# Branch B's fillers bound behind their scores, wo's norm from accumulated sums, other PSUM banks for down and wo

## The chip, the core and the metric

The kernel runs on one core of a Trainium2 chip. The metric is the device time of one execution in microseconds (us), lower is better. The kernel before takes 1801.39 us, the median of three runs (1801.26 to 1805.1).

A core has engines that run side by side, each through its own list of instructions in order: TensorE (PE, matmuls and transposes into PSUM banks), VectorE (DVE), ScalarE (ACT), GpSimd (POOL) and SyncE (SP, which issues DMAs). Semaphores make an instruction of one engine wait for one of another.

## What is computed

The reference is a two-layer encoder over 512 tokens of width 1024, all in fp32:

```python
for l in range(DEPTH):                                   # DEPTH = 2
    h = hybrid_mixer(x, ...)                             # branches A, B, C, gates, w_mix_out
    x = layer_norm(ALPHA * x + h, ln1_g[l], ln1_b[l])
    h = memory_cross_attention(x, mem, xwq, xwkv, xwo)   # 4 heads of 128, 256 memory tokens
    x = layer_norm(ALPHA * x + h, ln2_g[l], ln2_b[l])
    h = conv_ffn(x, ...)                                 # up to 2 x 2816, conv of 3, gelu(a) * b, down
    x = layer_norm(ALPHA * x + h, ln3_g[l], ln3_b[l])
```

Inside the mixer, branch B is the dense attention of 8 query heads over 2 key heads, with RMS-normed and rotated q and k:

```python
bq = rope2d(rms_norm(bq)); bk = rope2d(rms_norm(bk))
out_b = softmax(q @ k.T / sqrt(64)) @ v                  # all 512 positions
merged = sum_n (branch_n @ w_branch[n]) * sigmoid(gate_n + b_gate)
```

## The kernel before

**Matmuls.** The precision of fp32 is reached by splitting each operand into a high part (a copy to fp32r, line 133, ACT) and a low part (the rest, line 137, DVE). One product is three matmuls, `mm3` at lines 141 to 144: hi·hi (L142), hi·lo (L143), lo·hi (L144). Weights come in chunks of 128 x 1024 through a ring of raw tiles and five slots of split tiles w; `pump` loads and splits ahead, and a slot comes free when the last step that reads its chunk has run.

**Steps and the scheduler.** `layer` writes a list of steps; each step's `fn` issues its instructions. The scheduler that builds the program may move instructions of different steps past each other (it is run with a model of the engines' times), so the order of a list on PE is not the order of the steps. Two things constrain it: steps marked `urgent` get a higher priority, and an instruction given to `in_order` (`tc.keep_in_program_order`) keeps its place as written. SP's list is written by hand.

**Branch B.** For each of four token tiles t, `q_step` and `kv_step` project q, k and v, `rms` (L535, L536) and the power on POOL (L320) give the norm, L392 and L398 the rotation, L578 and L579 multiply, L133 and L137 split; then `qT_step` (L546) and `kT_step` (L594) transpose with PE, evicted by casts (L551, L595). All keys must be there before the first scores. Then 16 steps u (head u // 2, half of the queries u % 2), each with

- S(u), `bS_step`: for two query tiles q0 and q1 two matmuls into an s bank (two s banks in all), L699; the maximum on DVE (L701); exp on ACT into a ring slot (four slots); a reciprocal; a scaling on POOL
- T(u), `bT_step`: the transposes of the ring slots (L722) into a t bank, split by ACT and DVE into PTb
- PV(u), `bPV_step`: eight matmuls of 256 columns with V (L736); after every second one the pv bank is evicted through o (ACT, L128, then DVE, L666), split into brB.

S(u), T(u) and PV(u) hang on each other through ACT and DVE, so between them stand *fillers*: gate tiles (24 matmuls of 512 columns, acc<-w,xT or acc<-xT,w in the trace, with a Tanh into the ring tile) and branch products (12 matmuls, acc<-brA,w, evicted at L786). `fillers(0, 1)` gives 16 of them for branch A's share, one after each S(u). After the 16 steps come PV(14), T(15) and PV(15), with two gate tiles of branch B's share (`gB[0]`, `gB[1]`) between, then branch B's products (acc<-brB,w).

**wo and the norms.** `wo_step(t)` accumulates the output projection of the cross-attention for one token tile in two halves, each in an acc bank (three acc banks). `residual` (L355) adds it to ALPHA * x and takes bn_stats of the sum (L358); `ln_finish` aggregates (L363), adds the epsilon (L365), takes the power on POOL and applies (x - mean) * g and * rs + b on DVE (L369, L372). Then `xT_step(t)` transposes the tile (L346, two t banks) and splits it for the up projection.

**down and the layer boundary.** The second half of the down projection keeps four token tiles open: tiles 0 and 1 in acc banks, tiles 2 and 3 in the two t banks. The last chunks are done tile by tile (`down_t_step`), then the norm, and `xT_step(0)` and `xT_step(1)` of the next layer, whose transposes need t banks.

Of the kernel before, what the change touches and what calls it, by code (L numbers as in the profile page):

```python
# [10 lines left out]
F32 = mybir.dt.float32  # L11
F32R = mybir.dt.float32r
AF = mybir.ActivationFunctionType
# [3 lines left out]
P = 128  # L17
# [60 lines left out]
def encoder_kernel(ctx: ExitStack, tc: tile.TileContext, x_in, xt_in, mem_in, w_in, pp_in, ln_in, cln_in, ws_in, co_in, out):  # L78
# [27 lines left out]
    def acc_tile(n=512):  # L106
        return ps_acc.tile([P, 512], F32, tag="acc", name="acc")
# [7 lines left out]
    def t_tile(dt=F32):  # L115
        return ps_t.tile([P, 4, P], dt, tag="t", name="t")
# [10 lines left out]
    def act(out, in_, func=AF.Identity, **kw):  # L127
        return nc.scalar.activation(out, in_, func, **kw)  # L128
# [6 lines left out]
    def split_lo(out, in_, hi, scale=None):  # L135
        if scale is None:
            return nc.vector.tensor_tensor(out=out, in0=in_, in1=hi.bitcast(F32), op=ALU.subtract)  # L137
        return nc.vector.scalar_tensor_tensor(out=out, in0=in_, scalar=scale, in1=hi.bitcast(F32),
                                              op0=ALU.mult, op1=ALU.subtract)

    def mm3(ps, lh, ll, rh, rl, first, last):
        nc.tensor.matmul(ps, lhsT=lh, rhs=rh, start=first, stop=False)  # L142
        nc.tensor.matmul(ps, lhsT=lh, rhs=rl, start=False, stop=False)  # L143
        nc.tensor.matmul(ps, lhsT=ll, rhs=rh, start=False, stop=last)  # L144

# [214 lines left out]
    def ln_finish(t, g, b):  # L360
        st = ln_stats.pop(t)
        mv = sm(2, "mv")
        nc.vector.bn_aggr(out=mv, in_=st.rearrange("p a b -> p (a b)"))  # L363
        ve = sm(1, "ve")
        nc.vector.tensor_scalar_add(ve, mv[:, 1:2], LN_EPS)  # L365
        rs = rstd_of(ve, 1, "rs")
        for hf in range(2):
            xt = X[0][:, t, hf * 512:hf * 512 + 512]
            nc.vector.scalar_tensor_tensor(out=xt, in0=xt, scalar=mv[:, 0:1], in1=g[hf], op0=ALU.subtract, op1=ALU.mult)  # L369
        for hf in range(2):  # L370
            xt = X[0][:, t, hf * 512:hf * 512 + 512]
            nc.vector.scalar_tensor_tensor(out=xt, in0=xt, scalar=rs, in1=b[hf], op0=ALU.mult, op1=ALU.add)  # L372
# [33 lines left out]
    def layer(l):  # L406
# [348 lines left out]
        def gate_step(n, m):  # L755
# [8 lines left out]
                R["tg", n, m] = tg  # L764
            return Step(fn, [K("gate", i)])

        def br_step(n, m, stage):
            key = K("br", n * 4 + m // 2)

            def fn():  # L770
                ps = acc_tile()
                w = W.get(key, 2 * 4, P)
                br = R["ABC"[n]]
                for k in range(4):
                    mm3(ps, w[:, 0, (m % 2) * 4 + k, :], w[:, 1, (m % 2) * 4 + k, :],
                        br[:, 0, k, :], br[:, 1, k, :], k == 0, k == 3)
                pump()
                tg = R.pop(("tg", n, m))
                if stage == 0:
                    if m == 0:  # L780
                        R["mg"] = big_tile([P, KD, S], F32, "mg")
                    nc.vector.scalar_tensor_tensor(out=R["mg"][:, m, :], in0=tg, scalar=1.0, in1=ps,
                                                   op0=ALU.add, op1=ALU.mult)
                    return
                mg = R["mg"][:, m, :]
                nc.vector.scalar_tensor_tensor(out=tg, in0=tg, scalar=1.0, in1=ps, op0=ALU.add, op1=ALU.mult)  # L786
                nc.gpsimd.tensor_tensor(out=mg, in0=mg, in1=tg, op=ALU.add)
                if stage == 2:
                    if m == 0:
                        R["mh"] = big_tile([P, KD, S], F32R, "mh")  # L790
                        R["ml"] = big_tile([P, KD, S], F32R, "ml")
                    split_hi(R["mh"][:, m, :], mg, scale=0.5)
                    split_lo(R["ml"][:, m, :], mg, R["mh"][:, m, :], scale=0.5)
            return Step(fn, [key])
# [159 lines left out]
        def wo_step(t):  # L954
            chunks = [K("wo", c) for c in range(4)]

            def fn():
                if t == 0:
                    R["ln"] = load_ln(l, 1)
                ps = [acc_tile(), acc_tile()]  # L960
                sl = slice(t * P, (t + 1) * P)
                oT = R["oT"]
                for half, k in [(0, 0), (0, 1), (0, 2), (1, 0), (1, 1), (1, 2), (0, 3), (1, 3)]:
                    w = W.get(chunks[half * 2 + k // 2], 2, 512)
                    mm3(ps[half], oT[:, 0, k, sl], oT[:, 1, k, sl], w[:, 0, k % 2, :], w[:, 1, k % 2, :],
                        k == 0, k == 3)
                pump()
                for half in range(2):
                    residual(t, half, ps[half])
                ln_finish(t, *R["ln"])  # L970
            return Step(fn, chunks)


# [165 lines left out]
        def down_k_step(half, c):  # L1139
            def fn():  # L1140
                if c == 0:
                    if half == 0:
                        R["dn", 0] = [s_tile(), s_tile(), pv_tile(), acc_tile()]
                        gt = kv_p.tile([P, DM], F32, tag="v", name="ln3g", bufs=2)
                        bt = [p_tile(name="ln3b") for _ in range(2)]
                        R["ln"] = load_ln(l, 2, ([gt[:, :512], gt[:, 512:]], bt))
                    else:
                        R["dn", 1] = [acc_tile() for _ in range(2)] + [
                            t_tile().rearrange("p a b -> p (a b)") for _ in range(2)]
                if half == 0:  # L1150
# [28 lines left out]
        def st(s):  # L1179
            steps.append(s)  # L1180
# [25 lines left out]
                st(tc_step(2 * t - 2))  # L1206
                st(tc_step(2 * t - 1))
        fC, fA, fB = fillers(2, 0), fillers(0, 1), fillers(1, 2)
        for nm, fl in (("a", fC), ("b", fA)):
            if nm == "b":  # L1210
                st(q_step("b", 0))
                st(aT_step(15))
# [16 lines left out]
            for u in range(16):  # L1229
                st(S_(u))  # L1230
                if fl:
                    st(fl.pop(0))
                if nm == "a" and u >= 3 and u % 2 == 1:
                    st(aPV_step((u - 3) // 2))
                if nm == "b" and u >= 2:
                    st(bPV_step(u - 2))
                if u >= 1:
                    st(T_(u - 1))
            for f in fl:
                st(f)  # L1240
        gB = [f for f in fB[0::2]]
        pB = [f for f in fB[1::2]]
        fB = [gB[2]]
        for m in range(8):
            fB.append(pB[m])
            if m + 3 < 8:
                fB.append(gB[m + 3])
        st(gB[0])
        st(bPV_step(14))
        st(bT_step(15))  # L1250
        st(gB[1])
        st(bPV_step(15))
        for f in fB[:6]:
            st(f)
        add(load_x)
# [250 lines left out]
```

## Time and profile before

| | |
|---|---|
| median of three runs | 1801.39 us (1801.26 to 1805.1) |
| the profiled execution | 1802.87 us |
| its span | 1801.1 us |
| mean granted clock of PE | 0.997 |
| PE busy | 1770.0 us, 98% |
| DVE, ACT, POOL busy | 69%, 46%, 14% |

The profile is one execution. Its own time is 1.8 us over its span and 1.5 us over the median. In its rows, out<-in are the names of the tiles that an instruction writes and reads; L numbers are lines of the kernel. A row of the timeline gives start, duration, engine, line, operation, tiles and shapes, and in brackets the idle time of the engine just before with what ended it. A row of the stretches gives the length and then, for PE, PE's weight loads, DVE, ACT and POOL, the busy time and the instructions, then the clock granted to PE, the share of DMA and GB/s.

### The profile page before, as it was taken

The numbers are of one execution on the slowest core, as the hardware profiler recorded it, in microseconds if no ns is written. First come the engines' busy times: TensorE is split into PE (matmuls) and PEld (weight loads), VectorE is DVE, ScalarE is ACT, GpSimd is POOL, SyncE is SP. The second block draws the span as 40 slices with busy tenths as digits, with TensorE's granted clock in tenths as the row PEclk, the third lists the DMA queues.
The fourth block names the chain that finished last, engine by engine and source line by source line (L and its number), as shares of the span: only waits on it lengthen the run. The fifth ranks groups of instructions, "written<-read, shape, count | busy, mean of one in ns | idle before, by whom it ended". The sixth has DMA issues, their size and how long they took to land.

```text
span 1801.1 us, 26334 instructions
## 1 busy us (share of the span) xinstructions
PE 1770.0 (98%) x10081; PEld 1544.4 (86%) x10081; DVE 1247.0 (69%) x2061; ACT 833.6 (46%) x1426; POOL 258.2 (14%) x296
## 2 busy tenths in 40 slices
PE   9999999999999999999999999999999999999998
PEld 7888888878978999988788888888789789998886
DVE  6666856556687898973656668565575878988734
ACT  5355645542444565652223555455424345656520
POOL 2112422121110000000011124321201100000000
PEclk9999999999999999999999999999999999999999
DMA  6222231242423455553412322212333235656421
GB/s 239 94 71 72 70 94 50 68 141 93 154 92 99 128 163 151 163 175 94 151 54 96 92 71 71 82 59 82 118 118 128 82 106 146 164 138 173 133 90 47
DMA packets 63917, 198.79 MB, mean 110 GB/s; under 512 B 7088, under 2 KB 7600, under 8 KB 63536
## 3 DMA queue, kind: packets, MB, share of 16 engines
q1 hardware_dynamic: 53424, 166.20, 28.1%
q0 software_dynamic: 4032, 14.68, 4.8%
q10 hardware_dynamic: 6336, 16.23, 2.7%
q8 instruction: 79, 1.29, 0.3%
q14 instruction: 46, 0.38, 0.1%
HBM read 192.89 MB, written 4.19 MB: 109 GB/s over the span
## 4 chain that ended last, share of the span: by engine, by line
PE 80%; DMA 8%; DVE 7%; issue 3%; ACT 2%; SPq 0%; DVEq 0%; POOLq 0%; ACTq 0%
PE acc L142 19%; PE acc L144 19%; PE acc L143 19%; DMA raw<-in_w_dram 8%; DVE w L137 2%; PE pv L736 2%; PE s L699 2%; PE t L722 1%; DVE cv L1003 1%; PE s L142 1%; PE s L144 1%; PE s L143 1%; DVE cv L1005 1%; PE pv L681 1%; PE s L615 1%
## 5 line engine op out<-in xcount | busy, mean ns | idle before, releaser
L137 DVE TENSOR_TENSOR w<-raw,w 128x1024 fp32r<-128x1024 f32 x308 | 386.2, 1258 | 203.2 <-ACT w L133 198.1
L133 ACT ACTIVATE w<-raw 128x1024 fp32r<-128x1024 f32 x308 | 325.2, 1059 | 387.6 <-PE acc L144 222.0
L144 PE MATMUL acc<-xT,w 128*128 128x512 f32 (+1 forms) x672 | 257.2, 383 | 3.7 <-DVE w L137 3.7
L142 PE MATMUL acc<-xT,w 128*128 128x512 f32 (+1 forms) x672 | 257.1, 384 | 1.1 <-DVE cv L1005 1.1
L143 PE MATMUL acc<-xT,w 128*128 128x512 f32 (+1 forms) x672 | 256.0, 381 | 0.0
L144 PEld LDWEIGHTS acc<-xT,w 128*128 128x128 f32 x672 | 126.4, 188 | 27.5 <-DVE w L137 5.4
L142 PEld LDWEIGHTS acc<-xT,w 128*128 128x128 f32 x672 | 126.2, 188 | 22.1 <-ACT cv L128 1.5
L143 PEld LDWEIGHTS acc<-xT,w 128*128 128x128 f32 x672 | 126.5, 188 | 21.3
L142 PE MATMUL acc<-w,xT 128*128 128x512 f32 (+1 forms) x392 | 139.6, 358 | 1.9 <-ACT w L133 1.5
L144 PE MATMUL acc<-w,xT 128*128 128x512 f32 (+1 forms) x392 | 140.2, 359 | 0.0
L143 PE MATMUL acc<-w,xT 128*128 128x512 f32 (+1 forms) x392 | 139.5, 357 | 0.0
L320 POOL TENSOR_TENSOR rs<-ve,mhalf 128x1 f32<-128x1 f32 x32 | 31.8, 993 | 517.4 <-DVE ve L365 468.0
L1063 PE MATMUL t<-S,w 128*128 128x256 f32 x336 | 95.0, 283 | 0.0
L1064 PE MATMUL t<-S,w 128*128 128x256 f32 x336 | 95.0, 283 | 0.0
L1065 PE MATMUL t<-S,w 128*128 128x256 f32 x336 | 93.7, 283 | 0.0
L701 DVE TENSOR_REDUCE nm<-s 128x1 f32<-128x512 f32 x64 | 44.0, 688 | 64.0 <-PE s L699 63.8
L142 PEld LDWEIGHTS acc<-w,xT 128*128 128x128 f32 x392 | 74.2, 189 | 13.1 <-ACT w L133 2.0
L143 PEld LDWEIGHTS acc<-w,xT 128*128 128x128 f32 x392 | 74.5, 190 | 10.3
L144 PEld LDWEIGHTS acc<-w,xT 128*128 128x128 f32 x392 | 74.3, 190 | 10.1
L203 POOL DMA_DIRECT2D raw<-in_w_dram x28 | 24.7, 882 | 377.9 <-DVE h L1092 115.0
L133 ACT ACTIVATE xT<-t 128x512 fp32r<-128x512 f32 x40 | 22.5, 595 | 109.8 <-PE t L346 109.7
L634 POOL TENSOR_SCALAR ring<-ring,rsm 128x256 f32<-128x256 f32 (+1 forms) x64 | 41.7, 664 | 182.4 <-DVE rsm L632 141.9
(317 smaller groups left out, 4658.7 us busy)
## 6 DMA issues: line engine op xcount, KB each, us to landing
raw<-in_w_dram SPq DMA_DIRECT2D x264, 512.0 KB, 3.6
raw<-in_w_dram SPq DMA_DIRECT2D x56, 256.0 KB, 3.0
raw<-in_w_dram POOLq DMA_DIRECT2D x28, 512.0 KB, 7.2
ub<-in_w_dram SPq DMA_DIRECT2D x28, 256.0 KB, 3.6
lngb<-in_ln_dram ACTq DMA_DIRECT2D x16, 256.0 KB, 4.6
xraw<-in_xt_dram SPq DMA_DIRECT2D x8, 256.0 KB, 6.3
memr<-in_mem_dram ACTq DMA_DIRECT2D x2, 1024.0 KB, 4.8
x<-in_x_dram ACTq DMA_DIRECT2D x4, 512.0 KB, 6.9
```

What stands on the lines that cost most here:

```text
L133: return nc.scalar.activation(out, in_, AF.Copy, scale=scale)
L137: return nc.vector.tensor_tensor(out=out, in0=in_, in1=hi.bitcast(F32), op=ALU.subtract)
L142: nc.tensor.matmul(ps, lhsT=lh, rhs=rh, start=first, stop=False)
L143: nc.tensor.matmul(ps, lhsT=lh, rhs=rl, start=False, stop=False)
L144: nc.tensor.matmul(ps, lhsT=ll, rhs=rh, start=False, stop=last)
L634: nc.gpsimd.tensor_scalar(out=pr_t[qi], in0=pr_t[qi], scalar1=rs[:, qi:qi + 1], scalar2=0.0, op0=ALU.mult, op1=ALU.add)
L699: nc.tensor.matmul(ps, lhsT=R["Q"][:, h, q * P:(q + 1) * P], rhs=R["Kt"][:, kv * 2 + hl, :], start=hl == 0, stop=hl == 1)
L701: nc.vector.tensor_reduce(out=nm[:, qi:qi + 1], in_=ps, axis=AX.X, op=ALU.max, negate=True)
L736: nc.tensor.matmul(ps, lhsT=R["V"][:, kt, h // 4, :], rhs=PT[:, hl, kt, :], start=kt == 0 and hl == 0, stop=kt == NT - 1 and hl == 1, skip ...
L1063: nc.tensor.matmul(o, lhsT=wh, rhs=x(0, k), start=first and k == 0, stop=False, **f)
L1064: nc.tensor.matmul(o, lhsT=wh, rhs=x(1, k), start=False, stop=False, **f)
L1065: nc.tensor.matmul(o, lhsT=wl, rhs=x(0, k), start=False, stop=last and k == 3, **f)
```

## The change

Three edits.

**1. Branch B.** A step wrapped in `behind` sets a flag, and the next first matmul of an `mm3` is given to `in_order`: it keeps its written place behind the scores S(u) that stand ahead of it in the list. In branch B each of the fillers that follows a S(u) is wrapped so. The list of fillers gets one gate tile of branch B's share more (`gB[:1]`), so that each step has one, and at the end `gB[1]` is wrapped too and `gB[2]` is split in two parts of four chunks each (`gate_part`), one ahead of PV(15) and one behind it.

**2. The norm of wo.** The residual's addition gives the sum of its row as a second output (`accum_out`). In place of bn_stats and bn_aggr, ACT squares (x - mean) in two halves with an accumulated sum, and DVE makes the mean and variance from the sums. The two other norms of a layer are as they were.

**3. Banks.** In down's second half tiles 0 and 1 get the t banks, 2 and 3 acc banks. In wo every fourth half (first half of tiles 0 and 2) gets the pv bank in place of an acc bank.

```diff
+    def behind(step):
+        def fn():
+            pinned[0] = True
+            step.fn()
+        return Step(fn, step.chunks)
+
     def mm3(ps, lh, ll, rh, rl, first, last):
-        nc.tensor.matmul(ps, lhsT=lh, rhs=rh, start=first, stop=False)
+        ins = nc.tensor.matmul(ps, lhsT=lh, rhs=rh, start=first, stop=False)
+        if pinned[0]:
+            in_order(ins)
+            pinned[0] = False
...
+    def residual_sum(t, half, ps):
...
+        nc.vector.scalar_tensor_tensor(out=xs, in0=xs, scalar=ALPHA, in1=ps, op0=ALU.mult, op1=ALU.add,
+                                       accum_out=ln_stats[t][:, half:half + 1])
+
+    def ln_finish_sum(t, g, b):
+        st = ln_stats.pop(t)
+        nm, var = st[:, 2:3], st[:, 3:5]
+        nc.vector.tensor_scalar(out=nm, in0=st[:, 0:1], scalar1=st[:, 1:2], scalar2=-1.0 / DM, op0=ALU.add, op1=ALU.mult)
+        for hf in range(2):
+            act(p_tile(name="sq"), X[0][:, t, hf * 512:hf * 512 + 512], AF.Square, bias=nm, accum_out=var[:, hf:hf + 1])
+        ve = sm(1, "ve")
+        nc.vector.tensor_scalar(out=ve, in0=var[:, 0:1], scalar1=var[:, 1:2], scalar2=1.0 / DM, op0=ALU.add, op1=ALU.mult)
+        nc.vector.tensor_scalar_add(ve, ve, LN_EPS)
+        rs = rstd_of(ve, 1, "rs")
...
-                ps = [acc_tile(), acc_tile()]
+                ps = [acc_tile() if (2 * t + i) % 4 else pv_tile() for i in range(2)]
...
-                    residual(t, half, ps[half])
-                ln_finish(t, *R["ln"])
+                    residual_sum(t, half, ps[half])
+                ln_finish_sum(t, *R["ln"])
...
-                        R["dn", 1] = [acc_tile() for _ in range(2)] + [
-                            t_tile().rearrange("p a b -> p (a b)") for _ in range(2)]
+                        R["dn", 1] = [t_tile().rearrange("p a b -> p (a b)") for _ in range(2)] + [
+                            acc_tile() for _ in range(2)]
...
-        for nm, fl in (("a", fC), ("b", fA)):
+        gB, pB = fB[0::2], fB[1::2]
+        for nm, fl in (("a", fC), ("b", fA + gB[:1])):
...
                 if fl:
-                    st(fl.pop(0))
+                    f = fl.pop(0)
+                    st(behind(f) if nm == "b" else f)
...
-        st(gB[0])
+        st(behind(gB[1]))
         st(bPV_step(14))
         st(bT_step(15))
-        st(gB[1])
+        st(behind(gate_part(1, 2, 0)))
         st(bPV_step(15))
+        st(gate_part(1, 2, 1))
```

How this moves PE's instructions, at three places. In the rows, L142, L143 and L144 of the kernel before are L151, L155 and L156 of the changed one; L594 is L630, L699 is L735, L722 is L758, L346 is L358. "x4" is four instructions alike in a row.

At the start of branch B, PE before has this between the transposes of the third and fourth tile of k (ks); brA marks a branch product and acc<-xT,w a gate tile, both fillers:

```order
L594 MATMUL t<-ident_r,ks 128x128 x4
L143 MATMUL acc<-brA,w 128x512
L144 MATMUL acc<-brA,w 128x512
L142 MATMUL acc<-brA,w 128x512
L143 MATMUL acc<-brA,w 128x512
L144 MATMUL acc<-brA,w 128x512
L142 MATMUL acc<-xT,w 128x512
L143 MATMUL acc<-xT,w 128x512
L144 MATMUL acc<-xT,w 128x512
L594 MATMUL t<-ident_r,ks 128x128 x4
```

And the changed kernel has this from the last projection (acc<-xT,w) to the first filler (L582 transposes q):

```order
L156 MATMUL acc<-xT,w 128x512
L582 MATMUL t<-ident_r,qs 128x128 x8
L630 MATMUL t<-ident_r,ks 128x128 x16
L735 MATMUL s<-Kt,Q 128x512 x4
L151 MATMUL acc<-brA,w 128x512
```

All sixteen transposes of k and the first scores now stand in one piece, and every filler that stood among them stands behind.

In a later step of branch B, PE before has this between the transposes of the ring (L722) and the scores of the second query tile (the last row):

```order
L722 MATMUL t<-ident,ring 128x128 x3
L142 MATMUL acc<-brA,w 128x512
L143 MATMUL acc<-brA,w 128x512
L144 MATMUL acc<-brA,w 128x512
L142 MATMUL acc<-brA,w 128x512
L143 MATMUL acc<-brA,w 128x512
L144 MATMUL acc<-brA,w 128x512
L142 MATMUL acc<-xT,w 128x512
L699 MATMUL s<-Kt,Q 128x512 x2
```

And the changed kernel has this at the same kind of place:

```order
L758 MATMUL t<-ident,ring 128x128 x2
L735 MATMUL s<-Kt,Q 128x512 x2
L758 MATMUL t<-ident,ring 128x128 x4
L735 MATMUL s<-Kt,Q 128x512 x2
L151 MATMUL acc<-xT,w 128x512
```

The filler that stood between the two pairs of scores now stands behind both.

At the layer boundary, PE before reaches the first transposes of x within the last matmuls of down's tile 3, which is in a t bank (wa and xT belong to the next layer's first projection):

```order
L143 MATMUL t<-w,gs 128x512
L346 MATMUL t<-ident,x 128x128 x4
L144 MATMUL t<-w,gs 128x512
L142 MATMUL acc<-wa,xT 128x512
L143 MATMUL acc<-wa,xT 128x512
L346 MATMUL t<-ident,x 128x128 x8
```

And the changed kernel has its first transposes of x between down's tiles 2 and 3, both in acc banks now:

```order
L156 MATMUL acc<-w,gs 128x512
L358 MATMUL t<-ident,x 128x128 x8
L151 MATMUL acc<-w,gs 128x512
```

All eight transposes of tile 0 moved ahead of tile 3's 24 matmuls.

More of the change, by code (lines that the diff above doesn't have):

```diff
@@ L139, in split_lo @@
                                               op0=ALU.mult, op1=ALU.subtract)
+    pinned = [False]
+    def behind(step):
[3 more added lines that the diff above has]
+        return Step(fn, step.chunks)
     def mm3(ps, lh, ll, rh, rl, first, last):
-        nc.tensor.matmul(ps, lhsT=lh, rhs=rh, start=first, stop=False)
+        ins = nc.tensor.matmul(ps, lhsT=lh, rhs=rh, start=first, stop=False)
+        if pinned[0]:
+            in_order(ins)
+            pinned[0] = False
         nc.tensor.matmul(ps, lhsT=lh, rhs=rl, start=False, stop=False)
@@ L369, in ln_finish @@
             nc.vector.scalar_tensor_tensor(out=xt, in0=xt, scalar=mv[:, 0:1], in1=g[hf], op0=ALU.subtract, op1=ALU.mult)
+        for hf in range(2):
+            xt = X[0][:, t, hf * 512:hf * 512 + 512]
+            nc.vector.scalar_tensor_tensor(out=xt, in0=xt, scalar=rs, in1=b[hf], op0=ALU.mult, op1=ALU.add)
+    def residual_sum(t, half, ps):
+        xs = X[0][:, t, half * 512:(half + 1) * 512]
+        if half == 0:
+            ln_stats[t] = small.tile([P, 5], F32, tag="lns", name="lns", bufs=4)
+        nc.vector.scalar_tensor_tensor(out=xs, in0=xs, scalar=ALPHA, in1=ps, op0=ALU.mult, op1=ALU.add,
[4 more added lines that the diff above has]
+        nc.vector.tensor_scalar(out=nm, in0=st[:, 0:1], scalar1=st[:, 1:2], scalar2=-1.0 / DM, op0=ALU.add, op1=ALU.mult)
+        for hf in range(2):
+            act(p_tile(name="sq"), X[0][:, t, hf * 512:hf * 512 + 512], AF.Square, bias=nm, accum_out=var[:, hf:hf + 1])
[3 more added lines that the diff above has]
+        rs = rstd_of(ve, 1, "rs")
+        for hf in range(2):
+            xt = X[0][:, t, hf * 512:hf * 512 + 512]
+            nc.vector.scalar_tensor_tensor(out=xt, in0=xt, scalar=nm, in1=g[hf], op0=ALU.add, op1=ALU.mult)
         for hf in range(2):
@@ L765, in gate_step, with gate_part, fn @@
             return Step(fn, [K("gate", i)])
+        def gate_part(n, m, part):
+            i = n * 8 + m
+            def fn():
+                if part == 0:
+                    R["gp"] = acc_tile()
+                ps = R["gp"]
+                w = W.get(K("gate", i), KD, P)
+                for k in range(4 * part, 4 * part + 4):
+                    mm3(ps, w[:, 0, k, :], w[:, 1, k, :], xT[:, :, 0, k, :], xT[:, :, 1, k, :], k == 0, k == KD - 1)
+                pump()
+                if part == 1:
+                    tg = tg_slot(n, m)
+                    act(tg, R.pop("gp"), AF.Tanh, bias=hbias[:, i:i + 1], scale=0.5)
+                    R["tg", n, m] = tg
+            return Step(fn, [K("gate", i)])
         def br_step(n, m, stage):
@@ L1240, in layer @@
                 st(f)
-        gB = [f for f in fB[0::2]]
-        pB = [f for f in fB[1::2]]
-        fB = [gB[2]]
+        fB = []
         for m in range(8):
```

## Prediction

> **What bounds the kernel now.** I began with the page of the profile: busy time of each engine, then the chain that ended last.
>
> ```profile
> span 1801.1 us, 26334 instructions
> PE 1770.0 (98%) x10081; PEld 1544.4 (86%) x10081; DVE 1247.0 (69%) x2061; ACT 833.6 (46%) x1426; POOL 258.2 (14%) x296
> PE 80%; DMA 8%; DVE 7%; issue 3%; ACT 2%; SPq 0%; DVEq 0%; POOLq 0%; ACTq 0%
> ```
>
> TensorE (PE) sets the time: it has 31.1 us without work in 1801.1, and the chain runs through it. The change takes no matmul away and adds none, so it can only close gaps of PE or open new ones. The second view, the waits of PE, says which gaps there are to close:
>
> ```profile
> PE acc L142 <- ACT brB L133: 4.1, 2, 2.1
> PE acc L144 <- DVE w L137: 3.7, 3, 1.7
> PE pv L143 <- DVE xT L137: 2.9, 2, 1.5
> PE t L346 <- DVE x L355: 1.5, 1, 1.5
> PE acc L142 <- DVE x L355: 1.3, 4, 0.3
> PE acc L142 <- DVE ring L786: 0.6, 2, 0.3
> PE pv L736 <- DVE o L666: 0.5, 2, 0.3
> ```
>
> The columns are total us, times and the longest. The brB, ring and o rows are the end of branch B, once in each layer; the x and xT rows are the wo stage and the layer boundary. Everything that the change aims at is in these rows without the w row: 10.9 us in all. A gap that the change opens is weighed against that. The third view is the order in which each engine's instructions stand in the two built programs (shown above); it says where gaps open.
>
> **Start of branch B, in each layer.** Before the first scores S(0), PE must transpose q and k of all four token tiles, and each k passes through VectorE (DVE), ScalarE (ACT) and GpSimd. Before, the scheduler had put fillers (gate and branch A tiles) between these transposes:
>
> ```profile
> 229.29 0.45 PE L546 MATMUL t<-ident_r,qs 128*128 128x128 f32 x4
> 229.58 0.46 PE L142 MATMUL acc<-brA,w 128*128 128x512 f32 x1
> ...
> 237.76 0.46 PE L594 MATMUL t<-ident_r,ks 128*128 128x128 f32 x4
> ...
> 240.66 0.46 PE L594 MATMUL t<-ident_r,ks 128*128 128x128 f32 x4
> 240.96 0.47 PE L143 MATMUL acc<-brA,w 128*128 128x512 f32 x1
> ...
> 248.71 1.07 PE L699 MATMUL s<-Kt,Q 128*128 128x512 f32 x4
> ```
>
> With each filler now bound behind its step's scores, nothing stands between 229.58 and S(0) but 20 transposes in five groups, each 0.3 us (240.66 to 240.96), 1.5 us together. PE works in its written order, so it waits for the chain through the keys. That chain's rows on DVE:
>
> ```profile
> 230.58 1.23 DVE L137 TENSOR_TENSOR w<-raw,w 128x1024 fp32r<-128x1024 f32 x1 [0.22 <-ACT w L133]
> 231.95 0.42 DVE L137 TENSOR_TENSOR ks<-tk,ks 128x256 fp32r<-128x256 f32 x1
> 232.62 0.69 DVE L786 SCALAR_TENSOR_TENSOR ring<-ring,acc 128x512 f32<-128x512 f32 x1 [0.24 <-PE acc L144]
> 235.58 0.29 DVE L579 TENSOR_TENSOR tk<-tk,rs 128x128 f32<-128x128 f32 x1 [0.69 <-POOL rs L320]
> 236.65 0.41 DVE L137 TENSOR_TENSOR ks<-tk,ks 128x256 fp32r<-128x256 f32 x1
> 238.26 0.69 DVE L595 CAST Kt<-t 128x512 fp32r<-128x512 f32 x1 [1.20 <-PE t L594]
> ```
>
> The last key is ready at 237.06 (236.65 + 0.41). It waited for no filler's matmuls except through L786, which now comes later; in its place two casts of Kt (0.69 each) stand in DVE's row, so I take 237.1 to 237.3. Then a group of transposes and the handover (0.5 us, as from the group at 237.76 to its cast at 238.26), the cast 0.69 and a handover of 0.1 to 0.2: S(0) at about 238.6. PE then idles 238.6 - 229.58 - 1.5 = 7.5 us in each layer: **+15.0**. The fillers that stood there are not saved; they run later. Bounds: without the w row (1.23), the L786 row and the longer waits around them S(0) could come near 235.7 (4.6 us idle); with one more piece of 0.8 us in the chain, 8.3 us.
>
> **The clock after such a gap.** How PE's clock answers to idleness shows once in this trace, at the start (stretches: PE busy, then other engines, PEclk ahead of the last two columns; then rows of PE):
>
> ```profile
> 7.00:8.00 1.00, 0.61 (x2) 0.30 (x2) 1.00 (x2) 0.63 (x1) 0.00 (x0) 0.91 0.94 344
> 8.00:9.00 1.00, 1.00 (x3) 0.81 (x4) 0.88 (x2) 0.57 (x1) 0.00 (x0) 0.50 1.08 367
> 11.00:12.00 1.00, 1.00 (x5) 0.84 (x4) 0.95 (x2) 0.61 (x1) 0.00 (x0) 0.88 1.07 432
> ...
> 6.47 1.01 PE L142 MATMUL acc<-w,xT 128*128 128x512 f32 x2 [1.47 <-ACT w L133]
> 9.33 0.63 PE L142 MATMUL acc<-w,xT 128*128 128x512 f32 x1
> 9.75 0.63 PE L143 MATMUL acc<-w,xT 128*128 128x512 f32 x1
> 12.50 0.39 PE L142 MATMUL acc<-w,xT 128*128 128x512 f32 x1
> 12.73 0.39 PE L143 MATMUL acc<-w,xT 128*128 128x512 f32 x1
> ```
>
> After a stretch with an idle 1.47 us in it the granted clock was 0.50 from about 7.8 to 11.2 (0.91 and 0.88 in the mixed microseconds), 3.4 us, and matmuls of 512 columns followed each other by 0.42 us (9.33, 9.75) where 0.23 (12.50, 12.73) is usual. If a gap of 7.5 us does the same, eight matmuls at 0.42 lose 8 x 0.19 = 1.6 us in each layer: **+3.2**. Bounds: nothing, and two such stretches, +6.4.
>
> [...]
>
> **Steady state of branch B.** The order now sets T (second half of the step before), scores of the first half, T, scores of the second half, with no filler between; before, three to seven and more matmuls of fillers stood ahead of the second scores. There are two score banks; the second scores need the exp of the step before on that bank, and this exp needs its ring slot, which that T has just read:
>
> ```profile
> 306.75 0.49 PE L722 MATMUL t<-ident,ring 128*128 128x128 f32 x3
> 307.00 0.48 PE L699 MATMUL s<-Kt,Q 128*128 128x512 f32 x1
> ...
> 307.01 0.59 ACT L128 ACTIVATE o<-pv 64x512 f32<-64x512 f32 x1 [5.15 <-PE pv L736]
> 307.63 0.69 ACT L128 ACTIVATE ring<-s,nm 128x512 f32<-128x512 f32 x1
> 308.22 0.19 ACT L128 ACTIVATION_READ_ACCUMULATOR ring<-s,nm 128x1 f32 x1
> ```
>
> The last of the three T starts at about 306.86; the exp ends at 308.32 (307.63 + 0.69), 1.5 us later, with the eviction o (0.59) ahead of it on ACT, and about 1.1 without. PE gets there in 0.9: two score matmuls (2 x 0.23) and four transposes (0.45). So it waits 0.57 in the six steps that have o and some 0.16 in two others: 3.7 us in a layer. Besides, in the new ACT order a weight split waits, in one or two steps, for a slot that PE frees at a filler's end, with an exp queued behind it on ACT and the scores behind that; between 0 and 3 us, of which I take 0.7, since each such split is only about 1 us long. 4.4 in each layer: **+8.8**; bounds 2 and 8 in each. Before, PE's waits list nothing of this kind, so there is nothing to win there.
>
> **End of branch B.** The stretch from the last scores to the first tiles of branch B, in layer 0 (PE busy is the first number behind the length):
>
> ```profile
> 358.65:376.22 17.57, 14.73 (x83) 11.53 (x82) 10.57 (x15) 8.72 (x14) 4.12 (x4) 1.00 0.28 97
> ```
>
> PE lacks work for 2.84 us here, most of it the brB row's 2.06 (4.1 over two). Two gate tiles (48 matmuls) and part of a third now stand ahead of PV(15) and behind it, 5.4 us each, longer than the chain they cover. The transposes of the last step still wait for exp and ring; I leave 0.6. Gain 2.2 in each layer: **-4.4** (bounds -2 and -6.4).
>
> **Layer boundary, once.** The first xT step needs two t banks, and before, down's tile 3 held one:
>
> ```profile
> 897.96 0.50 PE L142 MATMUL acc<-wa,xT 128*128 128x512 f32 x1 [0.45 <-ACT xT L133]
> 900.21 1.32 PE L346 MATMUL t<-ident,x 128*128 128x128 f32 x8 [1.52 <-DVE x L355]
> ```
>
> Now tiles 0 and 1 hold them, whose residuals are done by then, and a whole down tile (24 matmuls) covers the split. Both waits go: **-2.0** (0 to -3.2).
>
> **Norm of the wo stage.** Per tile two bn_stats and an aggregate leave DVE, two Square passes with a sum go to ACT, and two small scalar steps come in:
>
> ```profile
> 892.37 0.69 DVE L358 BATCH_NORM_STATS2 bn<-x 128x6 f32<-128x512 f32 x1
> ```
>
> DVE is rid of about 2 x 0.69 a tile; a Square of that width, not in the trace, I estimate by the exp row with its read, 0.69 + 0.19, two a tile on an ACT that is 46% busy. But the Squares wait for the residual's sum and the scaling on DVE waits for the Squares, so the chain of one tile is no shorter. The bank swap takes the 0.3 us wait of wo (x row, four times) down a little, while xT(0) now stands behind all of wo's matmuls. I take -0.5 in each layer: **-1.0**, bounds -5 (all xT and x rows) and +4.
>
> **Sum.** 15.0 + 3.2 + 8.8 - 4.4 - 2.0 - 1.0 = +19.6. The profiled execution took 1802.87 us, 1.5 over the median of the three runs (1801.39); so 1822.5 by the profiled run, and **1821.0** against the median.
>
> **Rivals.** (1) Only the gaps at the start count: no slower clock, no waits in the steady state, all gains in full: 15.0 - 4.4 - 2.0 - 1.0 = +7.6, 1809. For it: waits on ACT as short as 0.6 may fall together with others. Against it: the order leaves no cover.
> (2) Faster: the chain through the keys is short as soon as DVE and ACT are rid of the fillers' evictions and splits. S(0) then comes at 235.7 in both layers, with 4.6 us idle, and the same relief takes o and the splits out of the exps' way: 9.2 with no steady waits, against gains at their ends (6.4 + 3.2 + 5.0 = 14.6): -5.4, 1796. It decides once start and steady state together cost less than the gains. Against it: POOL's 0.69 and the DVE rows of one token tile after another are the chain itself, and w's split is still in DVE's order ahead of ks.
> (3) No change: costs at their low ends (9.2 at the start, 4 in the steady state, no slow clock) meet gains near their high ends (11 to 14.6): 1799 to 1804.
> (4) The splits on ACT hold up the scores in every second step: 8 in each layer for 4.4, and the norm stage loses its 4: 19.6 + 7.2 + 5.0 = about +32, 1833 to 1834.
> (5) The slow clock lasts twice as long, about 6.8 us behind each gap, as PE resumes in the middle of a stretch that was already idle: sixteen matmuls at 0.42, 3.2 in each layer, so +22.8 in all, 1824. For it: at the start the clock fell at 7.8, after work had resumed at 6.47, so it follows its own stretches. Against it: there, one stretch was enough. [...]
>
> **Numbers.** Forecast (1811 to 1832) 0.51, the first rival 0.13, the fourth 0.06, the fifth 0.13: slower 0.83. The second, 0.10, is faster. The third, 0.07, lies within 0.2%, 3.6 us, which is about what a measurement of this kernel can tell from none. The range, 1803 to 1834, leaves out the faster case and the far ends.
>
> **What would show it.** Right: PE idle 7 to 8 us ahead of the first score matmuls of branch B, once in each layer, a granted clock of 0.50 behind each, waits of s on ACT's exp in later steps, and rows of brB and of t on x gone. The forecast is wrong if that first gap is under 4.6 us, or if the span grows elsewhere than between the first k transposes and the last exp of branch B.

## The result, and the profile after

The changed kernel takes 1816.87 us (median of four runs, 1814.23 to 1820.74) against 1801.46 us before: ratio 1.0087, 95% interval [1.0071, 1.0103], so 12.8 to 18.6 us slower. The forecast was 1821.0 with a range of 1803 to 1834. The profiled execution took 1814.23 us, its span 1812.5.

The page of the changed kernel, busy times and the chain that ended last:

```profile
span 1812.5 us, 26335 instructions
PE 1775.4 (98%) x10081; PEld 1547.4 (85%) x10081; DVE 1233.1 (68%) x2069; ACT 842.9 (47%) x1458; POOL 253.4 (14%) x296
PE 83%; DVE 7%; DMA 5%; issue 3%; ACT 2%; SPq 0%; POOL 0%; DVEq 0%; POOLq 0%; ACTq 0%
```

The matmuls are the same 10081; PE is without work for 37.1 us instead of 31.1, and its busy time grew by 5.4 us with no more work in it, at a mean granted clock of 0.993 instead of 0.997. The waits of PE in the changed kernel (us in total, times, longest):

```profile
PE t L630 <- ACT ks L133: 6.1, 2, 3.2
PE s L735 <- ACT ring L128: 5.6, 16, 0.4
PE t L358 <- DVE xT L137: 2.6, 2, 1.3
PE pv L772 <- ACT PTb L133: 2.4, 2, 1.2
PE t L630 <- DVE Q L587: 1.6, 2, 0.8
PE s L735 <- DVE Kt L631: 1.6, 2, 0.8
PE t L630 <- DVE Kt L631: 1.4, 2, 0.7
```

The old rows of brB, ring L786, o and x are gone. In their place stand two new families: transposes of k that wait for the chain through the keys (ks, Q, Kt), and 16 waits of scores on the exp into the ring. New are also the waits of PV on PTb at the end of branch B and of the transposes of x on the split xT in wo. The timeline of PE at the start of branch B in layer 0:

```profile
227.61 0.80 PE L582 MATMUL t<-ident_r,qs 128*128 128x128 f32 x8
229.20 0.54 PE L630 MATMUL t<-ident_r,ks 128*128 128x128 f32 x4 [0.79 <-DVE Q L587]
229.99 0.54 PE L630 MATMUL t<-ident_r,ks 128*128 128x128 f32 x4 [0.25 <-ACT Q L133]
231.22 0.86 PE L630 MATMUL t<-ident_r,ks 128*128 128x128 f32 x4 [0.70 <-DVE Kt L631]
235.06 1.08 PE L630 MATMUL t<-ident_r,ks 128*128 128x128 f32 x4 [2.98 <-ACT ks L133]
236.93 2.08 PE L735 MATMUL s<-Kt,Q 128*128 128x512 f32 x4 [0.78 <-DVE Kt L631]
238.80 0.63 PE L151 MATMUL acc<-brA,w 128*128 128x512 f32 x1
239.23 0.63 PE L155 MATMUL acc<-brA,w 128*128 128x512 f32 x1
...
241.81 0.39 PE L156 MATMUL acc<-brA,w 128*128 128x512 f32 x1
242.04 0.39 PE L151 MATMUL acc<-brA,w 128*128 128x512 f32 x1
```

From the transposes of q to S(0) pass 236.93 - 227.61 = 9.32 us, 5.5 of them shown as idle, the rest transposes that grew longer towards the end (1.08 us for four, 0.45 before). The rows behind S(0) show the clock: 0.43 us from matmul to matmul at 238.80, 0.23 at 241.81. The stretches around it in layer 0, then in layer 1 (the granted clock is the number ahead of the last two):

```profile
228.00:231.00 3.00, 1.49 (x13) 1.06 (x12) 2.55 (x5) 2.41 (x5) 0.35 (x1) 1.00 0.01 3
231.00:234.00 3.00, 0.86 (x4) 0.61 (x4) 2.53 (x10) 0.00 (x0) 0.52 (x1) 0.51 0.48 180
...
237.00:240.00 3.00, 3.00 (x7) 2.44 (x8) 1.38 (x2) 1.01 (x3) 0.00 (x0) 0.50 0.00 0
240.00:243.00 3.00, 3.00 (x12) 2.38 (x11) 0.25 (x2) 0.55 (x2) 1.36 (x2) 0.79 0.00 0
...
1132.00:1135.00 3.00, 0.41 (x2) 0.23 (x2) 1.68 (x6) 0.42 (x1) 0.69 (x1) 0.53 0.21 83
...
1138.00:1141.00 3.00, 3.00 (x9) 2.35 (x8) 1.17 (x3) 1.56 (x4) 0.65 (x1) 0.50 0.00 0
1141.00:1144.00 3.00, 3.00 (x11) 2.41 (x11) 0.87 (x2) 0.00 (x0) 0.81 (x3) 0.77 0.00 0
```

Worked out from the mixed stretches (0.51, 0.79; 0.53, 0.77), the clock is halved from 231.1 to 241.3 and from 1132.2 to 1142.4: 10.2 us both times, three times the 3.4 us seen at the kernel's start before.

Where the time went, as lengths of stretches between the starts of the same matmuls in both profiles (us):

| stretch of PE | before | changed | growth |
|---|---|---|---|
| layer 0, transposes of the last q to the first mix matmul (229.29 to 406.14, 227.61 to 415.92) | 176.85 | 188.31 | +11.5 |
| layer 1, the same | 176.84 | 189.02 | +12.2 |
| layer 0, first wo matmul to the last of the first up tiles | 54.39 | 54.13 | -0.3 |
| layer 1, the same | 55.61 | 54.12 | -1.5 |
| layer boundary, 200 matmuls from the 5001st on | 44.53 | 41.83 | -2.7 |
| all others: kernel's start, up and down stages | | | -7.8 |

Between the ends of each stretch of branch B PE has the same 896 matmuls in both kernels. The first five add up to +19.2. The others, in which instructions stand in the order of before, are taken up below.

### The profile page after: what moved, and what is told of

Read it like the earlier page. It is cut to its first block, busy times and chain, and to the rows that moved or that the text cites. A ratio compares the mean times of both kernels' runs of the same rounds, so it can differ in the third digit from the quotient of the medians.

```text
span 1812.5 us, 26335 instructions
## 1 busy us (share of the span) xinstructions
PE 1775.4 (98%) x10081; PEld 1547.4 (85%) x10081; DVE 1233.1 (68%) x2069; ACT 842.9 (47%) x1458; POOL 253.4 (14%) x296
## 4 chain that ended last, share of the span: by engine, by line
PE 83%; DVE 7%; DMA 5%; issue 3%; ACT 2%; SPq 0%; POOL 0%; DVEq 0%; POOLq 0%; ACTq 0%
PE acc L151 19%; PE acc L155 18%; PE acc L156 18%; DMA raw<-in_w_dram 5%; PE s L735 2%; PE pv L772 2%; DVE w L137 2%; PE t L1117 1%; PE t L1116 1%; PE t L1118 1%; PE s L155 1%; PE s L156 1%; PE s L151 1%; PE t L155 1%; PE t L151 1%
## 5 line engine op out<-in xcount | busy, mean ns | idle before, releaser
L151 PE MATMUL acc<-xT,w 128*128 128x512 f32 (+1 forms) x672 | 256.2, 382 | 0.7 <-DVE cv L1058 0.7
L156 PE MATMUL acc<-xT,w 128*128 128x512 f32 (+1 forms) x672 | 255.7, 381 | 0.6 <-DVE w L137 0.6
L155 PE MATMUL acc<-xT,w 128*128 128x512 f32 (+1 forms) x672 | 256.2, 382 | 0.0
L156 PEld LDWEIGHTS acc<-xT,w 128*128 128x128 f32 x672 | 126.4, 188 | 23.5 <-DVE w L137 1.1
L151 PEld LDWEIGHTS acc<-xT,w 128*128 128x128 f32 x672 | 126.2, 188 | 22.5 <-ACT cv L128 1.0
L155 PEld LDWEIGHTS acc<-xT,w 128*128 128x128 f32 x672 | 126.5, 188 | 21.7
L151 PE MATMUL acc<-w,xT 128*128 128x512 f32 (+1 forms) x392 | 139.1, 356 | 1.3 <-ACT w L133 0.9
L156 PE MATMUL acc<-w,xT 128*128 128x512 f32 (+1 forms) x392 | 139.7, 358 | 0.0
L155 PE MATMUL acc<-w,xT 128*128 128x512 f32 (+1 forms) x392 | 138.7, 355 | 0.0
L151 PEld LDWEIGHTS acc<-w,xT 128*128 128x128 f32 x392 | 74.0, 189 | 12.9 <-ACT w L133 1.9
L155 PEld LDWEIGHTS acc<-w,xT 128*128 128x128 f32 x392 | 74.0, 189 | 10.1
L156 PEld LDWEIGHTS acc<-w,xT 128*128 128x128 f32 x392 | 73.9, 189 | 10.0
L128 ACT ACTIVATE ring<-s,nm 128x512 f32<-128x512 f32 x64 | 44.3, 692 | 64.9 <-PE t L758 44.3
L1116 PEld LDWEIGHTS t<-S,w 128*128 128x128 f32 x336 | 64.5, 192 | 0.5
```

The source lines that it names most:

```text
L151: ins = nc.tensor.matmul(ps, lhsT=lh, rhs=rh, start=first, stop=False)
L1116: nc.tensor.matmul(o, lhsT=wh, rhs=x(0, k), start=first and k == 0, stop=False, **f)
```

## Experiments

Two theories were to be told apart. **A**, the forecast's: the loss is made in branch B by the pins, in three parts: the gap ahead of S(0), the slow clock behind it, and scores that wait on an exp with nothing in between; the other edits gain. **Rivals**: the other edits lose too, the rearranged list and not the pin is to blame, or the slowness has another cause. Times are medians; a ratio is to the runs of before on the same chip.

**Branch B's edit alone.** Norm and banks as before:

```diff
-                ps = [acc_tile() if (2 * t + i) % 4 else pv_tile() for i in range(2)]
+                ps = [acc_tile(), acc_tile()]
...
-                    residual_sum(t, half, ps[half])
-                ln_finish_sum(t, *R["ln"])
+                    residual(t, half, ps[half])
+                ln_finish(t, *R["ln"])
...
-                        R["dn", 1] = [t_tile().rearrange("p a b -> p (a b)") for _ in range(2)] + [
-                            acc_tile() for _ in range(2)]
+                        R["dn", 1] = [acc_tile() for _ in range(2)] + [
+                            t_tile().rearrange("p a b -> p (a b)") for _ in range(2)]
```

> Only edit 1, branch B's list and pins; norm and banks as before. Theory A (the loss lies in branch B: gap at its start, slow clock behind it, waits on exp): both branch B stages lose 11 to 13 us each as in the changed kernel, and the -2 to -4 of the other edits is missing, so 1817 to 1824, +18 to +22. Rival R (part of the loss comes from the Square passes of the norm on ScalarE or from the other banks): the time falls below 1813.

Measured: 1826.72 us, ratio 1.0134 [1.0114, 1.0154], 24.6 us above the 1802.12 of before there. This is 2.7 over theory A's upper end and far from the rival: the other edits don't lose. Its two stretches of branch B take 188.3 and 188.8 us, as in the changed kernel.

**The other two edits alone.** Branch B's list as before:

> Edits 2 and 3 alone, branch B as before. Theory A: the 2.0 us of idle time at the layer boundary go and wo gains 0 to 1 in each layer: -2 to -4, 1797.5 to 1799.5, and no gap at the start of branch B. Rival R: no faster than before, 1801 or more, since two Square passes per tile delay wo's norm.

Measured: 1797.12 us, ratio 0.9970 [0.9956, 0.9984]: 5.0 us faster, 1 more than expected at the upper end, with the interval reaching from 2.9 to 7.9. The layer boundary is 2.70 us shorter, as in the changed kernel.

**The changed list without pins.**

```diff
-                    st(behind(f) if nm == "b" else f)
+                    st(behind(f) if nm == "b" and False else f)
...
-        st(behind(gB[1]))
+        st(gB[1])
...
-        st(behind(gate_part(1, 2, 0)))
+        st(gate_part(1, 2, 0))
```

> The changed kernel without any pin: the list with one gate tile more and the split gate tile stay, but no filler is bound. Theory A (the pins make the loss, since the fillers that covered the key chain can no longer move ahead): no gap over 1 us at the start of branch B, the idle time at branch B's end back at 2 to 3 us in each layer, and 1797 to 1801. Rival L (the rearranged list, not the pin, moves the fillers): the gap at the start stays and the time is over 1808.

Measured: 1800.11 us, ratio 0.9993 [0.9982, 1.0004]. PE again has fillers between the transposes, and S(0) to S(1) is 6.35 us, as before at a granted clock of 1.00, so the pin is the cause and not the list. But from the last scores to the first mix matmul it takes 50.1 us in each layer where the kernel before takes 47.3. As many gate matmuls stand behind the last scores as before (76); what differs is the order of T and PV among them. PE waits 4.4 us there in layer 0 (358 to 377 us), not the 2 to 3 expected, where before has 2.7, and the granted clock is 0.72 from 372 to 378 us, which is 3.4 us at half, where before has 1.00. So the list alone makes branch B's end 2.9 us worse. With that the -5 of the other edits is nearly used up.

**The clock by itself.** Between the transposes of k stand short matmuls of a constant, whose results are overwritten:

```diff
+        def warm(n):
+            def fn():
+                ps, z = s_tile(), ident.bitcast(mybir.dt.bfloat16)
+                for _ in range(n):
+                    in_order(nc.tensor.matmul(ps[:, 0:256], lhsT=z[:, 0:P], rhs=z[:, 0:256], start=True, stop=True))
+            return Step(fn)
...
                     st(kT_step(t - 1))
+                    if nm == "b" and t > 1:
+                        st(warm(6 if t == 2 else 22))
             st(fl.pop(0))
             st(kT_step(3))
+            if nm == "b":
+                st(warm(5))
```

> The changed kernel with 33 short matmuls of constants (256 columns) placed among the key transposes, so that TensorE is not idle in the gap; their results are overwritten, nothing else is moved. It measures the clock's share alone. Theory A: the first scores start at the same time (within 0.6 us), the granted clock stays at 1.00 there, the 12 + 4 matmuls behind the gap take 3.7 us instead of 5.8, and the time falls by 2 to 3 us in each layer against the changed kernel: 1811 to 1813, with less spread from run to run. Rival W (the slowness behind the gap is not the clock's, or the clock falls all the same): 1815 or more.

The stretch with the gap and PE from S(0) on in layer 0, then two stretches of layer 1, in this run:

```profile
235.00:238.00 3.00, 2.33 (x22) 1.84 (x19) 1.81 (x9) 0.41 (x1) 0.69 (x1) 1.00 0.42 157
...
239.75 1.19 PE L735 MATMUL s<-Kt,Q 128*128 128x512 f32 x4 [0.22 <-DVE Kt L631]
240.78 0.39 PE L151 MATMUL acc<-brA,w 128*128 128x512 f32 x1
...
243.52 1.07 PE L735 MATMUL s<-Kt,Q 128*128 128x512 f32 x4
...
1135.00:1138.00 3.00, 2.97 (x19) 1.99 (x17) 2.81 (x10) 0.00 (x0) 0.24 (x1) 0.68 0.53 175
1138.00:1141.00 3.00, 3.00 (x23) 2.29 (x21) 1.11 (x3) 0.42 (x1) 0.46 (x1) 0.76 0.00 0
```

In layer 0 the clock stays at 1.00. In layer 1 it is halved once, worked out from the two mixed stretches from 1136.1 to 1139.4, among the short matmuls, and full again ahead of S(0) at 1141.35. With a full clock behind the gap S(0) to S(1) takes 243.52 - 239.75 = 3.77 us, in layer 1 3.76, where the changed kernel has 5.79 and 6.57; everything from S(1) to the last scores is the same to 0.05 us. So the halved clock costs 2.0 us in one layer and 2.8 in the other. S(0) comes 9.14 us after the transposes of q instead of 9.32 (layer 1: 9.46 instead of 9.31): the gap itself has almost nothing to do with the clock.

The whole time did not show the gain: 1816.52, ratio 1.0075 [1.0055, 1.0096], not told apart from 1.0087 and 3.5 us over theory A's upper end. By its number rival W would hold, and its second half did happen once, in layer 1; but wherever the clock was full the slowness behind the gap was gone. The profiled execution, the slowest of the four, shows where the gain went. Against the changed kernel's profile branch B takes 2.2 us less in layer 0 and only 1.0 less in layer 1, where its end holds another 3.4 us of half clock (1255.5 to 1258.9); the kernel's start and the wo, up and down stages, where nothing differs, take 8.7 us more. In layer 0's up and down stage PE waits 4.1 us (2.4 of them on one split of w), in the changed kernel's 0.5.

**Pinned behind the first scores only.** Each step's scores are two steps now, and the filler is bound between them:

```diff
-                st(S_(u))
-                if fl:
-                    f = fl.pop(0)
-                    st(behind(f) if nm == "b" else f)
+                if nm == "b":
+                    st(bS_half(u, 0))
+                    st(behind(fl.pop(0)))
+                    st(bS_half(u, 1))
...
```

> The changed kernel with each step's filler bound behind the first query tile's scores instead of both, so that filler work can lie between the two. It tests the cost in the steady state. Theory A (the second scores wait on the exp that the transposes before them release, with nothing in between): the 16 waits of 0.37 us of scores on ScalarE's exp go, first scores of step 1 to last scores of step 15 falls from 99.5 us to 96.5 to 97 in each layer, the gap and the slow clock at the start stay (S(0) to S(1) again 5.5 to 6.6 us): 1810 to 1813. Rival B (the scores wait for their PSUM bank and not for what stands between): the waits stay, 1815 or more.

Measured: 1805.55 us, ratio 1.0016 [1.0006, 1.0027], 11 us faster than the changed kernel and about twice the gain that theory A had said. The waits of PE in this kernel from S(0) of layer 0 to its mix stage:

```profile
PE s L735 <- DVE Kt L631: 0.8, 1, 0.8
PE pv L775 <- DVE PTb L137: 0.4, 1, 0.4
PE pv L775 <- ACT PTb L133: 0.3, 1, 0.3
PE t L761 <- DVE PTb L137: 0.2, 1, 0.2
```

And the same stretch of the changed kernel:

```profile
PE s L735 <- ACT ring L128: 2.8, 8, 0.4
PE pv L772 <- ACT PTb L133: 1.2, 1, 1.2
PE s L735 <- DVE Kt L631: 0.8, 1, 0.8
PE pv L772 <- DVE PTb L137: 0.3, 1, 0.3
```

The eight waits on exp are gone. From S(1) to the first mix matmul this kernel takes 167.83 us, the changed one 173.20: 5.4 less in each layer. What the eight waits cost can be read from the starts of matmuls in the changed kernel:

```profile
267.89 0.60 PE L758 MATMUL t<-ident,ring 128*128 128x128 f32 x4
268.86 0.72 PE L735 MATMUL s<-Kt,Q 128*128 128x512 f32 x2 [0.37 <-ACT ring L128]
```

From the start of the four transposes to the start of the scores pass 0.97 us; at 254.11, where the scores do not wait, 0.35. So this wait costs 0.62 us, not 0.37. A single transpose has a row of 0.27 us, but a score that does not wait starts 0.03 us after the start of the transpose ahead of it (249.41 and 249.44); the idle time in brackets counts only from the end of the transposes' row (267.89 + 0.60 = 268.49, and 0.37 to 268.86). All eight cost 4.75 us in a layer, where the view shows 2.8. The waits at the end of branch B, read in the same way, cost 2.04 us in the changed kernel and 1.55 here, which makes 5.2 of the 5.4. My mistake was in the expectation, which took the shown waits for the whole cost. That the time from S(1) to the last scores did not get shorter (100.2 against 99.5) is no contradiction, since more filler lies ahead of the last scores now. In layer 1 the slow clock lasted only 6.8 us here (1129.5 to 1136.4), which is part of the gain in time.

**Two fillers left free at the start.** On top of that, 36 matmuls may move ahead of the last key, and one more gate tile is taken into the list:

```diff
-        for nm, fl in (("a", fC), ("b", fA + gB[:1])):
+        for nm, fl in (("a", fC), ("b", fA + gB[:2])):
...
-            st(fl.pop(0))
+            for _ in range(3 if nm == "b" else 1):
+                st(fl.pop(0))
             st(kT_step(3))
...
-        st(behind(gB[1]))
+        st(behind(gB[2]))
-        st(behind(gate_part(1, 2, 0)))
+        st(behind(gate_part(1, 3, 0)))
```

> As the run before, with two fillers (36 matmuls, 8.2 us) left unbound ahead of the last key transposes, and one gate tile of branch B's share more in the list, so that 15 steps still have a filler and two gate tiles are kept for the end. Theory A (what the start needs is cover for 7.5 us, the rest of the fillers is free to be bound): under 1 us idle at the start, clock 1.00, no waits on exp but in the last, unfilled step (1 us), end of branch B as in the changed kernel, so against before 2.7 us at the boundary, some 0.7 in wo and 1 to 2.5 in branch B: 1794 to 1797.5. Rival C (the fillers that stood at the start were all needed there): 1800 or more.

> As the run before with three fillers (48 matmuls, 11 us) left unbound at the start and two steps near the end without one. Theory A: no gap at the start, 2 to 3 us of waits in the two unfilled steps in each layer: 1796 to 1800, 1 to 4 slower than the run before. Rival C: faster than the run before by 2 or more.

> The version with two unbound fillers at the start once more, on the chip of the two others: 1794 to 1797. Theory A: 1 to 1.5 us slower than the same with acc banks in wo; rival E: 1 us or more faster than that.

Measured: 1795.24 us with two free fillers, ratio 0.9955 [0.9943, 0.9968], and on another chip 1793.89, 0.9952 [0.9934, 0.9969]; with three 1795.31, 0.9953 [0.9938, 0.9968]. Both beat the kernel before and the changed one; between two and three there is no difference, against the expectation of 1 to 4 us. PE's waits in branch B with two free fillers (225 to 425 us):

```profile
PE s L735 <- DVE Kt L631: 1.0, 1, 1.0
PE pv L775 <- DVE PTb L137: 0.9, 1, 0.9
PE t L761 <- POOL ring L747: 0.6, 1, 0.6
PE pv L775 <- ACT PTb L133: 0.4, 1, 0.4
```

The gap of 7.5 us is 1.0, the mean granted clock 0.998 where the changed kernel has 0.993, and 36 matmuls of cover are enough, not the 75 of before. Yet from the last transpose of q to mix branch B takes 173.4 us (405.90 - 232.47), before 173.5 (406.14 - 232.63): its 2.9 us of waits stand where before had 2.7. By these two profiles branch B gains nothing by pins, even good ones; what this version has over the kernel before comes from the other two edits. One small thing may speak for the pins: in three of the ten stretches of branch B in kernels with the old list and no pins, a 3.4-us piece of half clock at the end made it 1.1 to 1.4 us longer, in none of the eight with free fillers and pins. Such small numbers do not show it.

**The norm alone, and wo's banks.**

> Only the norm of wo from accumulated sums, all banks and branch B as before; one look, read from the trace from wo's first matmul to the up projection. Theory A (the Square passes have room on ScalarE, and the chain of a tile is no shorter): that stretch within 0.7 us of before, each Square 0.6 to 0.7 us and an accumulator read of 0.2. Rival D (the norm alone brings wo's gain): 1 us or more shorter in each layer.

The waits of PE in wo and xT, with the norm alone (505 to 560 us):

```profile
PE acc L151 <- DVE x L390: 0.9, 2, 0.6
PE pv L151 <- ACT xT L133: 0.5, 2, 0.3
PE pv L155 <- DVE xT L137: 0.2, 1, 0.2
```

And in the changed kernel with the pv bank (515 to 567 us):

```profile
PE t L358 <- DVE xT L137: 1.3, 1, 1.3
PE pv L155 <- DVE xT L137: 0.6, 1, 0.6
PE pv L151 <- ACT xT L133: 0.2, 1, 0.2
```

The Square passes take 0.716 us each with a read of 0.188. From wo's first matmul to the last of the first up tiles it takes 53.37 and 53.42 us, before 54.39 and 55.61, and with branch B's edit alone 55.89 and 54.43. In the kernel before, layer 1's stretch holds a piece of half clock:

```profile
1433.00:1436.00 3.00, 1.22 (x5) 1.02 (x6) 3.00 (x6) 0.00 (x0) 0.00 (x0) 0.77 0.00 0
1436.00:1439.00 3.00, 3.00 (x19) 3.00 (x19) 2.93 (x7) 0.00 (x0) 0.92 (x1) 0.67 0.00 0
```

That is 3.4 us at half, from 1434.6 to 1438.0, and the 55.89 has such a piece too (553.2 to 556.6). So the norm brings 1.0 by the waits, which is rival D, and the one run took 1797.02 us. Another 1.2 to 1.5 us come where it spares the slow clock: of the six stretches with the old norm (three kernels) four hold such a piece, of the 22 with the norm from sums (eleven kernels) none. With the pv bank the stretch is 54.13: the bank swap moves the transposes of x behind all of wo, where they wait for a t bank (1.3 us, the first of the rows above for the changed kernel), and gives 0.7 us back in each layer.

> The version with two unbound fillers at the start and the pins behind the first scores, but wo's halves in acc banks as before; norm from sums and down's banks as changed. Theory A (in wo the sums gain and the pv bank gives it back: the look at the norm alone had TensorE waiting 1.6 us in wo and xT where the changed kernel has 2.1 and before had 2.7): wo's first matmul to the first up tiles 0.5 to 0.8 us shorter in each layer than with the pv bank, so 1 to 1.5 us faster than that version, 1793 to 1795. Rival E (the pv bank is what brings wo's gain): 1 us or more slower than that version.

> The norm from sums and down's banks alone, wo in acc banks, branch B as before. Theory A: against before -2.7 at the boundary and -1.0 in wo in each layer: 1796 to 1798.5. Rival E: 1799 or more.

Measured: 1792.10 us, ratio 0.9954 [0.9937, 0.9970], for the version with two free fillers and acc banks in wo, and 1795.31, 0.9961 [0.9945, 0.9976], for norm and down's banks alone. The stretch is 53.36 and 53.42 us with acc banks, 54.11 and 54.15 with the pv bank, as theory A has it; the 1.5 us in all do not stand out of the intervals of the whole time (0.9954 against 0.9952).

**down's banks alone, and the waits of the up stage.**

> Only down's banks as changed; norm, wo and branch B as before. It tells whether the shorter waits of the up projection, in profiles of kernels with the norm from sums 1.6 to 6.3 us of TensorE waits in both layers against 7.2 and 7.4 in two without it, come from the norm or from chance. Both theories: 2.7 us less at the layer boundary. Theory N (the norm's relief of VectorE reaches the weight splits of the up projection): waits of the up and down stretches (560 to 885 and 1455 to 1800 us) at 6 us or more, time 1799 to 1801. Rival Z (chance between runs): waits 2 to 5 us as in the others, 1796 to 1799.

Measured: 1799.80 us, ratio 0.9990 [0.9977, 1.0003], and 2.72 us less at the boundary. The waits in the two up and down stretches are 3.1 us, not 6 or more. That is rival Z's number while the time is theory N's. Of the 7.4 of branch B's edit alone, 2.6 were waits of its wo stage, which lies later there and reached into the window; and the run with short matmuls, which has the new norm, had 6.3. So these waits vary by chance, and the norm as their cause is not shown. What the old norm does cost here is in the wo stage: 55.91 and 55.90 us, both layers with a piece of half clock.

## Why the prediction was right

**The gap at the start**, +15.0: S(0) was put 9.31 us behind the transposes of q (238.6 - 229.29); it came 9.32 behind them, in layer 1 9.31. The chain held: in the changed kernel's DVE list casts of Kt took the place of the L786 row and of a cast of Q, and the w split stayed.

```profile
229.26 1.22 DVE L137 TENSOR_TENSOR w<-raw,w 128x1024 fp32r<-128x1024 f32 x1
230.39 0.68 DVE L631 CAST Kt<-t 128x512 fp32r<-128x512 f32 x1
230.99 0.41 DVE L137 TENSOR_TENSOR ks<-tk,ks 128x256 fp32r<-128x256 f32 x1
...
235.04 0.42 DVE L137 TENSOR_TENSOR ks<-tk,ks 128x256 fp32r<-128x256 f32 x1 [0.54 <-ACT ks L133]
236.18 0.69 DVE L631 CAST Kt<-t 128x512 fp32r<-128x512 f32 x1 [0.72 <-PE t L630]
```

Rival (2), a chain that shrinks once the fillers' work is out of the way, fell with this: S(0) would have come 6.4 us after the transposes.

**The clock**, +3.2: direction right, size too small. The granted clock was 0.50 behind each gap as forecast, but for longer than the 3.4 us that it took over from the kernel's start: S(0) at 236.93 still had 4.4 us of slow clock ahead, S(0) at 1136.36 6.0 us, since they came at different points of two stretches of the same length. The two layers pay 2.0 and 2.8, together 4.8. Rival (5) had 6.8 us of slow clock behind each gap, and half of the 3.2 us that it adds came. The prediction said that the clock's answer shows once in the profile before; it shows a second time, in wo (1434.6 to 1438.0, the rows above). There it fell within an idle 1.47 us, and the work that resumed at 1435.16 had 2.8 us of slow clock left, not 3.4: in these cases the cost went with the point at which the work resumed.

**The steady state**, +8.8: eight waits in each layer were forecast, six longer and two shorter, and so they came; by the starts they cost 4.75 in each layer, 9.5. Six have the eviction o ahead of the exp on ACT, as forecast, and cost 0.61 to 0.68 each, not 0.57. In the two others a weight split that had waited 3.8 us for PE and a Tanh stand ahead of the exp without a gap (in layer 0 at 289.62, 290.59 and 291.16): that is the head-of-line wait of the forecast, and they cost 0.47 each, where it had 0.16 each and 0.7 besides. So the mechanism was right, the six 0.4 too small in a layer and the rest 0.1 too large.

**The end of branch B**, -4.4: by the starts of matmuls, as for the eight waits (what a step from start to start takes beyond the usual one between two such matmuls), PE loses 4.05 us behind the last scores in the kernel before and 2.04 in the changed one, in each layer, so -4.0. In the view 1.5 us of waits are left in layer 0 (the two rows of PV on PTb), not the 0.6 that the prediction left. By subtraction, 11.5 - 7.5 - 2.0 - 4.75 + 2.0 = -0.75 in layer 0 and 12.2 - 7.5 - 2.8 - 4.75 + 2.0 = -0.85 in layer 1 remain: 1.6 us that branch B gains somewhere else, and where is not shown.

**The boundary**, -2.0: -2.7, the same in every kernel with down's banks changed; a wait of 0.45 and one of 1.52 cost more than they show, as above. **wo**, -1.0: -0.3 and -1.5, of which 1.2 is the piece of half clock that only the kernel before has; the step was right that the Squares and the scaling wait for one another, but wrong that the bank swap helps, and it left out the clock.

**The sum.** 15.0 + 4.8 + 9.5 - 4.0 - 1.6 - 2.7 - 1.8 = +19.2 by stages, +19.6 in the forecast. Single terms were off by up to 1.6 us, in both directions; that their sum comes within 0.4 is luck in part. The time grew by 15.4, interval 12.8 to 18.6. The other stretches of the profiled execution add -7.8 to its growth, which makes it 11.4: the kernel's start 1.7, the rest in the up and down stages. In the fourteen profiles of this document's kernels the start (to the transposes of the last q) takes 227.6 to 230.6 us with the same matmuls, the up and down stage 321.1 to 326.0 us in layer 0 and 327.3 to 331.7 in layer 1. The changed kernel has the shortest start and the shortest stage in layer 0, the kernel before the longest in layer 1: that is chance of two profiles. Branch B's edit alone and the other two alone add up to 24.6 - 5.0 = 19.6, near the stages' sum. What of the 4 us between these and the medians is not chance stays open.

## What to carry to other kernels

A pin keeps a filler behind a point, and so also out of the gaps ahead of it: before binding, look which chain the scheduler had covered with that work, and leave as much of it free as the chain is long (here 36 matmuls for 7.5 us). Look at the granted clock behind a gap: here 7.5 us of gap cost another 2.0 and 2.8 us. Bind filler between the two halves of a step and not behind it, when the second half waits for a slot that the instructions just ahead of it release (here eight waits, 4.75 us in a layer). Read the cost of a wait from the starts of the instructions around it, since the idle time shown can be less (here 0.37 us for 0.62).

## What was not expected of the hardware

A gap of 7.5 us of scattered idleness and transposes halved the clock for 10.2 us, in both layers; 33 short matmuls of a constant in each layer among the transposes kept it at 1.00 in layer 0 and let it fall for 3.4 us in layer 1. No long idle time stood ahead of the fall: in layer 0, at 231.1, PE had been idle for 0.79, 0.25 and about 0.6 us since the last transposes of q, in layer 1, at 1132.2, for 0.78, 0.26, 0.70 and about 0.9, and in wo of the kernel before, at 1434.6, for 0.25, 0.34 and about 0.9 behind the transposes of x at 1431.07. Eight waits of scores, 2.8 us in the view of waits, cost 4.75 us of time. An ACTIVATE with Square of 128x512 and its sum took 0.716 + 0.188 us, on DVE the sum of a residual a read of 0.083.
